# Gate units of block 2 as pairs of half-size products, with gates and results kept in DRAM

## The chip, the core and the metric

The kernel runs on one core of a Trainium2 chip. The metric is device time in microseconds, the median of several runs; lower is better.

## The reference, cut to what matters

Two blocks of two layers each run one after the other on 512 tokens of width 1024, in fp32. The change touches the second block. Its layer normalises the tokens and (in the first layer, for its output too) 256 context tokens, multiplies them with one wide matrix, runs three branches on parts of the product, and merges them:

```python
def merge_branches(ys, gm, w_br, w_out):
    y = jnp.stack(ys, axis=2)
    proj = jnp.einsum('btnw,nwd->btnd', y, w_br)
    g = jax.nn.sigmoid(gm.reshape(gm.shape[:2] + (N_BRANCH, -1)))
    return jnp.sum(g * proj, axis=2) @ w_out
```

Here `ys` are the results of branch a (differential attention, 4 heads), b (a bidirectional mLSTM, 4 heads) and c (neighbourhood attention, 4 pairs of heads), each 512 wide, and `gm` is a part of the wide product, 3 x 1024 columns: the gates.

## The kernel before, in words

Activations lie transposed: channels on the partitions, tokens on the free axis. A unit is 128 output channels, its weights one load of 512 KB. To keep fp32 accuracy, every operand is split in a high half of the type float32r and a low half (the rest); `mm3` (line 587) makes three matmuls per 128 channels of depth: high with high, high with low, low with high. So a unit over 1024 channels is 24 matmuls per block of up to 512 tokens. The normalised tokens are kept in `H` and `L` (high and low), 512 tokens and 256 of context. In layer 0 (`full`) a gate unit covers all 768, in layer 1 only the 512. `wload` (line 571) brings weights: a DMA on SyncE's queue into a buffer ws, a copy to the high half wh on ScalarE, a subtraction to the low half wl on VectorE; there are three buffers of each.

Block 2 (`run`, line 1817) goes through twelve heads in the order c, a, b. Each has a preparation and an attending (or scanning) generator. `weave` (line 492) runs the attending of one head beside the preparation of the next, in fixed proportions, and further generators beside them: `first` (the mLSTM's gates) and, by the table `MERGE` (line 1139), units of `merge` (line 1698). A unit of `merge` is a gate unit, its tanh on ScalarE and `branch_sum` (line 1721): 12 matmuls per block of tokens with the branch's weights (256 KB), multiplied with the gate and added to the sum `mg`. For branches c and a, 16 units stand beside heads 7 to 11; the 8 of branch b come after all heads. `out_proj` (line 1733) follows. Results of heads are split in high and low and stay in SBUF until their merge.

Working tiles come from the pool "s": 36 slots of 128 x 776 in block 2. PSUM tiles "P" are 8 banks.

What is written is not the order in which it is issued. `Order` (line 200) records every operation and in `flush` (line 371) orders them by a list schedule with modelled costs: each engine takes, of its first ready candidates in program order, the one that starts first, if its buffers are free; a tile may overtake others of its tag only by a set number (`AHEAD`, `WINDOW`). All instructions therefore carry line 486 (or 488, for runs that stay together) in the profile, and are told apart by their tiles: P is a PSUM tile, s a slot, wh and wl weights, H and L the split tokens.

Of the kernel before, what the change touches and what calls it, by code (L numbers as in the profile page):

```python
# [9 lines left out]
F32 = mybir.dt.float32  # L10
F32R = mybir.dt.float32r
I32 = mybir.dt.int32
AF = mybir.ActivationFunctionType
# [478 lines left out]
def weave(*gens):  # L492

    live = [[0.5 / n, 1.0 / n, g] for n, g in gens]
    while live:
        x = min(live, key=lambda x: x[0])
        x[0] += x[1]
        if next(x[2], live) is live:
            live.remove(x)


def chain(*gens):

    def run():
        for _, g in gens:
            yield from g
    return sum(n for n, _ in gens), run()


def some(g, n):  # L510

    for _ in range(n):
        next(g)
        yield

class Kern:
    WST = 3
# [30 lines left out]
    def part(self, o, n):  # L550
        return [self.H[:, k, o:o + n] for k in range(8)], [self.L[:, k, o:o + n] for k in range(8)]
# [19 lines left out]
    def wload(self, src, kt=8, m=128, parts=1):  # L571
        nc = self.nc
        self.n_ += 1
        w = kt * m
        st = nc.tile(self.wp, [128, 1088], F32, "wst", self.WST, f"ws{self.n_}")
        hi = nc.tile(self.wp, [128, 1088], F32R, "whi", 3, f"wh{self.n_}")
        lo = nc.tile(self.wp, [128, 1088], F32R, "wlo", 3, f"wl{self.n_}")
        src = src.rearrange("p k m -> p (k m)")
        for i in range(parts):
            r = slice(i * w // parts, (i + 1) * w // parts)  # L580
            nc.sync.dma_start(out=st[:, r], in_=src[:, r])
            nc.scalar.activation(hi[:, r], st[:, r], AF.Copy)
            nc.vector.tensor_tensor(lo[:, r], st[:, r], hi[:, r].bitcast(F32), op=ALU.subtract)
        return (hi[:, :w].rearrange("p (k m) -> p k m", k=kt),
                lo[:, :w].rearrange("p (k m) -> p k m", k=kt))

    def mm3(self, ps, w, xh, xl, order=None, start=True, stop=True):

# [547 lines left out]
VADD = (6, 7)  # L1136
FIRST = 7

MERGE = (0, 0, 0, 0, 0, 0, 0, 3, 3, 3, 4, 3)


class Block2:
# [83 lines left out]
    def source(self, name, j):  # L1226
# [4 lines left out]
            at += WN.get(u, 512) // 128  # L1231
        return self.A[f"w2in{self.l}"][at + j]

    def unit(self, name, j, lat, ctx):
        e = self.early.pop((self.l, name, j), None)
        if isinstance(e, list):
            return e
        return self.proj(self.source(name, j) if e is None else e, lat, ctx)
# [14 lines left out]
    def silu2(self, p):  # L1253

        nc = self.nc
        t = self.s(p[-1][1] + p[-1][2])
        for q, o, n in p:
            d = t[:, o:o + n]
            nc.scalar.activation(d, q, AF.Tanh, scale=0.5)
            nc.vector.scalar_tensor_tensor(d, d, 1.0, q, op0=ALU.add, op1=ALU.mult)  # L1260
        return t

    def ysplit(self, y, n):
        h, l = self.s(n, F32R), self.s(n, F32R)
# [15 lines left out]
    def head_out(self, o, ntile, g, gate):  # L1280

        K, nc = self.K, self.nc
        n = ntile * 128
        sq = self.s(n)
        b3 = lambda a: a.rearrange("p (a b) -> p a b", b=128)
        ss, v = K.tiny(ntile), K.tiny(ntile)
        nc.scalar.activation(sq, o, AF.Square)
        nc.vector.tensor_reduce(ss, b3(sq), axis=AX.X, op=ALU.add)
        nc.vector.tensor_scalar(v, ss, 1.0 / 128, EPS, op0=ALU.mult, op1=ALU.add)
        r = K.rsqrt(v, ntile)  # L1290
        nc.gpsimd.tensor_tensor(b3(o), b3(o), r.unsqueeze(2).to_broadcast([128, ntile, 128]), op=ALU.mult)
        for q, b, m in self.transposes(o, [i * 128 for i in range(ntile)]):
            d = gate[:, b:b + m]
            nc.vector.scalar_tensor_tensor(d, q, g, d, op0=ALU.mult, op1=ALU.mult)
        return self.ysplit(gate, n)


    def branch_a(self, lat, ctx, full, out):
# [50 lines left out]
        def attend(h):  # L1349
            st, vt = heads.pop(h)  # L1350
            nlam, gv = par
            o = self.s(ntile * 128)
            for t in range(ntile):
                isl = t < 4
                nk = 768 if isl else 256
                sm = K.tiny(4)
                mx = K.tiny(4)
                e = []
                for c in range(2):
                    S = K.pts(nk)  # L1360
                    for a, (q_, b, n) in enumerate(S):
                        k0 = b if isl else 512
                        K.mm_stack(q_, st[c], slice(t * 128, (t + 1) * 128), slice(k0, k0 + n))
                        nc.vector.tensor_reduce(mx[:, 2 * c + a:2 * c + a + 1], q_, axis=AX.X, op=ALU.max)
                    nm = K.tiny(1)
                    if isl:
                        nc.vector.tensor_scalar(nm, mx[:, 2 * c:2 * c + 1], mx[:, 2 * c + 1:2 * c + 2], -0.125,
                                                op0=ALU.max, op1=ALU.mult)
                    else:
                        nc.vector.tensor_scalar(nm, mx[:, 2 * c:2 * c + 1], -0.125, None, op0=ALU.mult)  # L1370
                    e.append(self.s(nk))
                    for a, (q_, b, n) in enumerate(S):
# [12 lines left out]
                O = K.pt(128)  # L1385
                for i in range(n):
                    nc.tensor.matmul(O, lhsT=pT[:, i * 128:(i + 1) * 128], rhs=vt[:, i if isl else 4 + i],
                                     start=(i == 0), stop=(i == n - 1))
                nc.scalar.activation(o[:, t * 128:(t + 1) * 128], O, AF.Copy)
                yield  # L1390
            z = self.silu2(self.unit("az", h, lat, cq))
            yield
            out.append(self.head_out(o, ntile, gv, z))

        return [((5 if h % 2 == 0 else 2, prep(h)), (ntile + 1, attend(h))) for h in range(4)]

# [80 lines left out]
    def branch_b(self, lat, ctx, full, out):  # L1477
# [33 lines left out]
        def scan(h):  # L1511
# [85 lines left out]
            out.append(self.head_out(o[0], ntile, gv, z))  # L1597

        return [((5 if h == 2 else 2, prep(h)), (6, scan(h))) for h in range(4)], (3, first())

# [1 line left out]
    def branch_c(self, lat, ctx, full, out):  # L1602
# [31 lines left out]
        def attend(j):  # L1634
# [58 lines left out]
            out.append(self.ysplit(y, nq))  # L1693

        return [((3, prep(j)), ((6 if full else 4) + 1, attend(j))) for j in range(4)]


    def merge(self, b, Y, mg, lat, ctx, full, last=False):


        K, nc, l = self.K, self.nc, self.l
        n = 768 if full else T
        cq = ctx if full else None
        late = []
        for m in range(8):
            t = self.s(n)
            for p, o, e in self.unit("gm", 8 * b + m, lat, cq):
                nc.scalar.activation(t[:, o:o + e], p, AF.Tanh, scale=0.5)
            late.append((mg, m, b, t, Y, n))
            if len(late) > (2 if last else 0):  # L1710
                self.branch_sum(*late.pop(0))
            yield
        for a in late:
            self.branch_sum(*a)
        if last:
            for m in range(8):
                h = K.H[:, m, :n]
                nc.scalar.activation(h, mg[m], AF.Copy, scale=0.5)
                nc.vector.scalar_tensor_tensor(K.L[:, m, :n], mg[m], 0.5, h.bitcast(F32), op0=ALU.mult, op1=ALU.subtract)
# [97 lines left out]
    def run(self, out, dbg, es):  # L1817
# [3 lines left out]
        for l in range(2):  # L1821
# [9 lines left out]
            early = chain((8, self.merge(2, yc, mg, lat, ctx, full)), (8, self.merge(0, ya, mg, lat, ctx, full)))[1]  # L1831
            weave(heads[0][0])
            for i in range(12):
                weave(heads[i][1], *([heads[i + 1][0]] if i < 11 else []), *([first] if i == FIRST else []),
                      *([(MERGE[i], some(early, MERGE[i]))] if MERGE[i] else []))
            weave((8, self.merge(1, yb, mg, lat, ctx, full, True)))
            X, S = self.out_proj(full, None if full or dbg == 6 else out)
            if dbg == 5 + l:
                for m in range(8):
# [43 lines left out]
```

## Time and profile before

| | us |
|---|---|
| median of 3 runs (lowest to highest) | 2919.61 (2916.12 to 2919.76) |
| the profiled execution | 2918.08 |
| its span, first to last instruction | 2916.3 |
| TensorE busy | 2868.6 |
| VectorE busy | 1876.1 |
| ScalarE busy | 1259.5 |
| GpSimd busy | 239.1 |

The first 1115 us or so are block 1; layer 0 of block 2 runs to about 2120 us, layer 1 to the end. The mean granted TensorE clock was 0.994 of full speed. A matmul's length in the profile is modelled and overlaps the next one's; the distance between starts is the rate. Idle time of an engine that is not the bottleneck costs nothing.

### The profile page before, as it was taken

How to read it: one execution, taken by the hardware profiler on the slowest of the kernel's cores; microseconds unless marked ns; L12 is line 12 of the kernel's file. 1: busy time of each engine (PE TensorE's matmuls, PEld its weight loads, DVE VectorE, ACT ScalarE, POOL GpSimd, SP SyncE). 2: the span in 40 equal slices, each digit the busy share in tenths (PEclk: the TensorE clock that was granted, in tenths of full speed). 3: DMA queues.
4: the chain of work that ended last, by engine and by line, in shares of the span. 5: the costliest groups of instructions: out<-in, count | busy, mean ns of one | idle time of the engine just before them, and what ended most of it. 6: DMA issues, size and time to landing. Idle time of an engine off the chain costs nothing.

```text
span 2916.3 us, 40946 instructions
## 1 busy us (share of the span) xinstructions
PE 2868.6 (98%) x15978; PEld 2432.4 (83%) x15978; DVE 1876.1 (64%) x3774; ACT 1259.5 (43%) x2405; POOL 239.1 (8%) x184
## 2 busy tenths in 40 slices
PE   8999999999999999999999999999999999999998
PEld 6788888887888888888888888888888888888887
DVE  7778678469786875656865554542466686565645
ACT  6344234455442443755554332322246555443324
POOL 1010000010100011000100101110100011011002
PEclk9999999999999999999999999999999999999999
DMA  4333433332334423111111212122222111132232
GB/s 148 119 120 129 136 133 118 104 102 81 129 110 140 141 94 123 66 64 44 37 34 41 87 56 66 60 89 71 91 95 82 45 58 42 66 95 79 87 105 87
DMA packets 94802, 260.58 MB, mean 89 GB/s; under 512 B 9608, under 2 KB 23304, under 8 KB 94608
## 3 DMA queue, kind: packets, MB, share of 16 engines
q1 hardware_dynamic: 94464, 257.96, 26.3%
q8 instruction: 125, 2.05, 0.3%
q14 instruction: 69, 0.57, 0.1%
q10 hardware_dynamic: 144, 0.00, 0.0%
HBM read 251.29 MB, written 6.64 MB: 88 GB/s over the span
## 4 chain that ended last, share of the span: by engine, by line
PE 92%; DVE 5%; DMA 1%; ACT 1%; issue 1%; POOL 0%; SPq 0%; DVEq 0%; ACTq 0%; POOLq 0%
PE P L486 91%; DVE s L486 2%; DVE t L486 1%; PE P L488 1%; DMA s<-cmd 1%; ACT s L486 1%; DVE tn L486 1%; DVE wl L486 1%; ACT wh L486 0%; DMA V<-in_vec 0%; DMA X<-in_x 0%; POOL t L486 0%; ACT t L486 0%; SPq L486 0%; DMA cmd<-s 0%
## 5 line engine op out<-in xcount | busy, mean ns | idle before, releaser
L486 PE MATMUL P<-H,wl 128*128 128x512 f32 (+1 forms) x2936 | 1079.6, 368 | 8.3 <-DVE wl L486 8.2
L486 PE MATMUL P<-H,wh 128*128 128x512 f32 (+1 forms) x2936 | 1081.2, 369 | 3.5 <-ACT s L486 1.9
L486 PE MATMUL P<-L,wh 128*128 128x512 f32 (+1 forms) x2936 | 1079.4, 368 | 1.5 <-DVE L L486 1.5
L486 ACT ACTIVATE wh<-ws 128x1024 fp32r<-128x1024 f32 (+4 forms) x426 | 412.1, 968 | 874.7 <-PE P L486 749.0
L486 DVE TENSOR_TENSOR wl<-ws,wh 128x1024 fp32r<-128x1024 f32 (+4 forms) x426 | 478.7, 1125 | 380.1 <-ACT wh L486 364.1
L486 PEld LDWEIGHTS P<-H,wl 128*128 128x128 f32 x2936 | 554.6, 189 | 104.7 <-DVE wl L486 10.3
L486 PEld LDWEIGHTS P<-H,wh 128*128 128x128 f32 x2936 | 554.5, 189 | 99.7 <-ACT s L486 3.0
L486 PEld LDWEIGHTS P<-L,wh 128*128 128x128 f32 x2936 | 554.2, 189 | 98.1 <-DVE L L486 3.2
L486 ACT ACTIVATE s<-P 128x512 f32<-128x512 f32 (+2 forms) x484 | 216.7, 479 | 330.6 <-PE P L486 307.3
L486 PE MATMUL P<-t,wh 128*128 128x512 f32 x960 | 301.3, 395 | 0.7 <-ACT t L486 0.7
L486 PE MATMUL P<-s,s 128*128 128x256 f32 (+4 forms) x1616 | 242.5, 290 | 6.0 <-DVE s L486 4.1
L486 PEld LDWEIGHTS P<-s,s 128*128 128x128 f32 (+1 forms) x1616 | 211.3, 188 | 31.2 <-ACT s L486 8.0
L486 PEld LDWEIGHTS P<-t,wh 128*128 128x128 f32 x960 | 180.6, 188 | 42.9 <-ACT t L486 0.9
L486 POOL TENSOR_TENSOR s<-s,s 128x512 f32<-128x512 f32 (+3 forms) x87 | 112.2, 1298 | 1155.2 <-DVE s L486 687.6
L486 PE MATMUL P<-t,wl 128*128 128x512 f32 x480 | 189.4, 395 | 0.0
L486 DVE TENSOR_REDUCE tn<-P 128x1 f32<-128x512 f32 (+1 forms) x224 | 105.9, 493 | 93.4 <-PE P L486 93.0
L486 DVE TENSOR_TENSOR s<-s,s 128x512 f32<-128x512 f32 (+6 forms) x173 | 148.4, 862 | 25.9 <-ACT s L486 12.3
L486 ACT ACTIVATE s<-s 64x768 fp32r<-64x768 f32 (+7 forms) x162 | 109.1, 680 | 119.0 <-DVE s L486 113.4
L486 PE MATMUL P<-s,wh 128*128 128x512 f32 (+1 forms) x576 | 155.6, 358 | 0.0
L486 DVE SCALAR_TENSOR_TENSOR t<-t,V,t 128x511 f32<-128x511 f32 (+1 forms) x196 | 148.3, 761 | 3.5 <-ACT t L486 1.6
L486 ACT ACTIVATE t<-t 128x512 f32<-128x512 f32 (+4 forms) x162 | 97.8, 611 | 112.1 <-DVE t L486 111.5
L486 PE MATMUL P<-wh,H 128*128 128x256 f32 (+2 forms) x512 | 145.9, 285 | 0.0
(142 smaller groups left out, 3114.8 us busy)
## 6 DMA issues: line engine op xcount, KB each, us to landing
ws<-in_w2in SPq DMA_DIRECT2D x136, 512.0 KB, 3.3
ws<-in_up SPq DMA_DIRECT2D x88, 512.0 KB, 3.2
wm<-in_w_mod SPq DMA_DIRECT2D x48, 512.0 KB, 4.2
ws<-in_down SPq DMA_DIRECT2D x32, 384.0 KB, 3.1
ws<-in_w2br SPq DMA_DIRECT2D x48, 256.0 KB, 2.6
ws<-in_down SPq DMA_DIRECT2D x32, 320.0 KB, 2.9
ws<-in_w0in SPq DMA_DIRECT2D x18, 512.0 KB, 3.4
ws<-in_w2out SPq DMA_DIRECT2D x16, 512.0 KB, 3.2
```

The source lines that it names most:

```text
L486: o["f"](*o["a"], **o["k"])
L488: f(*a, **k)
```

## The change

The 24 gate units of a layer are computed in pairs by a scheme with seven products in place of eight (Strassen's, in Winograd's form). The two units are the two halves of the output, the depth is cut in two halves of 512 channels and the tokens in two halves of n (384 in layer 0, 256 in layer 1). `halves`, once a layer, woven beside head 0, makes four combinations of token blocks (GpSimd restores fp32, VectorE subtracts, both split) and keeps them. `wpair` loads the pair's weights and makes four combinations of weight blocks on GpSimd. `pair` runs seven products of 12 matmuls of n columns, each added from PSUM on VectorE into the two outputs. `gm_pair` then takes the tanh and writes the gates to DRAM. The pairs stand beside heads 3 to 11 by the table `GM`. Results of branches c and a go to DRAM unsplit (`keep`). All three merges come after the heads: they load results and gates back and do the branch sums. There are four wh and wl buffers in place of three, and a smaller scratch for DMA descriptors of the GpSimd queue.

```diff
-        hi = nc.tile(self.wp, [128, 1088], F32R, "whi", 3, f"wh{self.n_}")
-        lo = nc.tile(self.wp, [128, 1088], F32R, "wlo", 3, f"wl{self.n_}")
+        hi = nc.tile(self.wp, [128, 1088], F32R, "whi", 4, f"wh{self.n_}")
+        lo = nc.tile(self.wp, [128, 1088], F32R, "wlo", 4, f"wl{self.n_}")
...
+    def wpair(self, srcs):
...
+        for i, src in enumerate(srcs):
+            st = nc.tile(self.wp, [128, 1088], F32, "wst", self.WST, f"ws{self.n_}_{i}")
+            nc.sync.dma_start(out=st[:, :1024], in_=src.rearrange("p k m -> p (k m)"))
+            raw.append(st)
...
+        sub = lambda o, x, y: nc.gpsimd.tensor_tensor(o, x, y, op=ALU.subtract)
+        put(raw[0], ("a11", "a12"))
+        sub(a11, a11, a21)
+        sub(s2, a22, a11)
+        put(s2, ("s2",), ("w2h", "w2l", 512, 1))
+        sub(a12, a12, s2)
+        put(raw[0], ("s3", "s4"))
+        nc.gpsimd.tensor_tensor(a21, a21, a22, op=ALU.add)
+        put(raw[1], ("s1", "a22"))
...
-MERGE = (0, 0, 0, 0, 0, 0, 0, 3, 3, 3, 4, 3)
+GM = (0, 0, 0, 1, 1, 1, 1, 2, 2, 2, 1, 1)
...
+    def halves(self, n):
...
+        for k in range(4):
+            x, y = self.s(2 * n), self.s(2 * n)
+            for a, r in ((x, k), (y, k + 4)):
+                nc.gpsimd.tensor_tensor(a, K.H[:, r, :2 * n].bitcast(F32), K.L[:, r, :2 * n].bitcast(F32), op=ALU.add)
...
+            nc.vector.tensor_tensor(b11, b12, b11, op=ALU.subtract)
+            nc.vector.tensor_tensor(b12, b22, b12, op=ALU.subtract)
+            nc.vector.tensor_tensor(b22, b22, b11, op=ALU.subtract)
+            nc.vector.tensor_tensor(b21, b21, b22, op=ALU.subtract)
+            for a, names in ((x, ("t1", "t3")), (y, ("t4", "t2"))):
+                h, l = self.ysplit(a, 2 * n)
...
+    def pair(self, srcs, o0, o1):
...
+        def part(a, b):
+            p = K.pt(n)
+            x = self.tk[b]
+            K.mm3(p, w[a], [q[0] for q in x], [q[1] for q in x])
+            return p
...
+        nc.scalar.activation(p1, part("a11", "b11"), AF.Copy)
+        yield
+        add(o0[:, n:], part("s2", "t2"), p1)
+        yield
+        add(o1[:, n:], part("s3", "t3"), o0[:, n:])
...
+    def gm_pair(self, b, m):
...
+        o = [self.s(2 * n) for _ in range(2)]
+        yield from self.pair([self.source("gm", 8 * b + m + i) for i in range(2)], *o)
+        for i in range(2):
+            nc.scalar.activation(o[i], o[i], AF.Tanh, scale=0.5)
+            nc.sync.dma_start(out=self.gd[b][:, m + i, :2 * n], in_=o[i])
+        yield
...
+    def keep(self, y, n, out, b):
+
+        if b == 1:
+            out.append(self.ysplit(y, n))
+        else:
+            self.nc.sync.dma_start(out=self.yd[b][:, len(out), :n], in_=y)
+            out.append(None)
...
         n = 768 if full else T
-        cq = ctx if full else None
-        late = []
+        for j in range(4):
+            if Y[j] is None:
+                y = self.s(n)
+                nc.sync.dma_start(out=y, in_=self.yd[b][:, j, :n])
+                Y[j] = self.ysplit(y, n)
         for m in range(8):
             t = self.s(n)
-            for p, o, e in self.unit("gm", 8 * b + m, lat, cq):
-                nc.scalar.activation(t[:, o:o + e], p, AF.Tanh, scale=0.5)
-            late.append((mg, m, b, t, Y, n))
-            if len(late) > (2 if last else 0):
-                self.branch_sum(*late.pop(0))
-            yield
-        for a in late:
-            self.branch_sum(*a)
+            nc.sync.dma_start(out=t, in_=self.gd[b][:, m, :n])
+            self.branch_sum(mg, m, b, t, Y, n)
...
+            gm = [self.gm_pair(b, m) for b in (2, 0, 1) for m in range(0, 8, 2)]
+            n = 384 if full else 256
             weave(heads[0][0])
             for i in range(12):
+                g = [gm.pop(0) for _ in range(GM[i])]
                 weave(heads[i][1], *([heads[i + 1][0]] if i < 11 else []), *([first] if i == FIRST else []),
-                      *([(MERGE[i], some(early, MERGE[i]))] if MERGE[i] else []))
-            weave((8, self.merge(1, yb, mg, lat, ctx, full, True)))
+                      *([(4, self.halves(n))] if i == 0 else []),
+                      *([chain(*((8, x) for x in g))] if g else []))
+            for b, y in ((2, yc), (0, ya), (1, yb)):
+                self.merge(b, y, mg, full, b == 1)
...
-    nc = bacc.Bacc("TRN2", target_bir_lowering=False, num_devices=1)
+    nc = bacc.Bacc("TRN2", target_bir_lowering=False, num_devices=1, dynamic_dma_scratch_size=1024)
```

## Rows read from the trace of the kernel before

**Rows 1.** The page's busy time: busy us, share of the span, instructions, by engine.

```profile
span 2916.3 us, 40946 instructions
PE 2868.6 (98%) x15978; PEld 2432.4 (83%) x15978; DVE 1876.1 (64%) x3774; ACT 1259.5 (43%) x2405; POOL 239.1 (8%) x184
```

**Rows 2.** The page's chain that ended last, by engine.

```profile
PE 92%; DVE 5%; DMA 1%; ACT 1%; issue 1%; POOL 0%; SPq 0%; DVEq 0%; ACTq 0%; POOLq 0%
```

**Rows 3.** Timeline of TensorE in layer 0: start us, modelled length us, instruction.

```profile
1899.92 0.40 PE L486 MATMUL P<-H,wh 128*128 128x512 f32 x1
...
1904.59 0.40 PE L486 MATMUL P<-H,wl 128*128 128x512 f32 x1
1904.82 0.28 PE L486 MATMUL P<-H,wh 128*128 128x256 f32 x1
...
1907.54 0.28 PE L486 MATMUL P<-H,wl 128*128 128x256 f32 x1
```

**Rows 4.** Stretches of heads: without merge work (first two), with it (last two).

```profile
core 0: us, PE busy (x) PEld busy (x) DVE busy (x) ACT busy (x) POOL busy (x), PEclk, DMA share, GB/s
1305.00:1505.00 200.00, 192.63 (x1325) 172.94 (x1325) 143.41 (x337) 107.80 (x273) 21.50 (x16) 0.99 0.12 41
2265.00:2440.00 175.00, 170.01 (x1145) 149.67 (x1143) 121.72 (x287) 94.41 (x234) 22.55 (x16) 1.00 0.15 52
1505.00:1950.00 445.00, 439.75 (x2759) 393.25 (x2758) 237.06 (x509) 151.99 (x328) 42.61 (x29) 1.00 0.19 63
2440.00:2755.00 315.00, 312.48 (x1741) 267.82 (x1742) 195.12 (x430) 132.12 (x278) 31.40 (x26) 1.00 0.23 75
```

**Rows 5.** Groups by form: a weight load.

```profile
L486 PEld LDWEIGHTS P<-H,wl 128*128 128x128 f32 x2936 | 554.6, 189 | 104.7 <-DVE wl L486 10.3 <-issue 1.2
```

**Rows 6.** Groups by form on VectorE, ScalarE, GpSimd: busy us, mean ns of one.

```profile
L486 DVE TENSOR_TENSOR wl<-ws,wh 128x1024 fp32r<-128x1024 f32 x304 | 374.5, 1232 | 236.9 <-ACT wh L486 225.1 <-PE P L486 9.0 <-ACT s L486 1.0
L486 DVE TENSOR_TENSOR wl<-ws,wh 128x512 fp32r<-128x512 f32 x52 | 38.1, 737 | 94.0 <-ACT wh L486 89.9 <-PE P L486 3.9
L486 DVE TENSOR_TENSOR s<-P,tn 128x384 f32<-128x384 f32 x16 | 8.2, 553 | 0.7 <-PE P L486 0.3 <-DVE tn L486 0.3
L486 DVE TENSOR_TENSOR s<-P,tn 128x256 f32<-128x256 f32 x16 | 6.1, 420 | 0.3
L486 DVE SCALAR_TENSOR_TENSOR s<-s,P 128x512 f32<-128x512 f32 x72 | 49.3, 685 | 68.0 <-PE P L486 48.0 <-ACT s L486 19.6
L486 ACT ACTIVATE wh<-ws 128x1024 fp32r<-128x1024 f32 x304 | 322.1, 1060 | 613.5 <-PE P L486 521.8 <-issue 88.1 <-ACT s L486 2.0
L486 ACT ACTIVATE wh<-ws 128x512 fp32r<-128x512 f32 x52 | 32.6, 630 | 111.9 <-PE P L486 95.0 <-issue 16.0 <-ACT s L486 0.9
L486 POOL TENSOR_TENSOR s<-s,s 128x512 f32<-128x512 f32 x53 | 73.7, 1394 | 940.3 <-DVE s L486 601.6 <-ACT s L486 163.3 <-DMA s<-xd 79.4
```

**Rows 7.** Timeline of GpSimd, then of VectorE, in layer 0.

```profile
1643.78 1.84 POOL L486 TENSOR_TENSOR s<-s,C 128x768 f32<-128x768 f32 x1 [1.03 <-DVE s L486]
1644.15 2.56 DVE L486 TENSOR_TENSOR wl<-ws,wh 128x1024 fp32r<-128x1024 f32 x1
```

**Rows 8.** DMA issues: KB each, median us to landing.

```profile
ws<-in_w2br SPq DMA_DIRECT2D x48, 256.0 KB, 2.6
s<-xd SPq DMA_DIRECT2D x16, 256.0 KB, 4.4
```

**Rows 9.** Groups by form on VectorE: making a head's stacked operands.

```profile
L486 DVE TENSOR_TENSOR s<-s,s 64x768 fp32r<-64x768 f32 x48 | 46.5, 969 | 3.1 <-ACT s L486 1.8
L486 DVE CAST s<-s 64x768 fp32r<-64x768 f32 x32 | 20.4, 665 | 0.7
```

**Rows 10.** Waits: who waited for whom, us in total, times, longest.

```profile
PE P L486 <- DVE wl L486: 8.2, 5, 3.4
SPq L486 <- DVE wl L486: 2039.8, 363, 28.2
```

More of the change, by code (lines that the diff above doesn't have):

```diff
@@ L507, in chain @@
     return sum(n for n, _ in gens), run()
-def some(g, n):
-    for _ in range(n):
-        next(g)
-        yield
 class Kern:
@@ L585, in wload, with put @@
                 lo[:, :w].rearrange("p (k m) -> p k m", k=kt))
+    def wpair(self, srcs):
+        nc = self.nc
+        self.n_ += 1
+        raw = []
+        for i, src in enumerate(srcs):
+            st = nc.tile(self.wp, [128, 1088], F32, "wst", self.WST, f"ws{self.n_}_{i}")
+            nc.sync.dma_start(out=st[:, :1024], in_=src.rearrange("p k m -> p (k m)"))
+            raw.append(st)
+        s2 = nc.tile(self.wp, [128, 512], F32, "w2", 1, f"w2{self.n_}")
+        a11, a12, a21, a22 = (raw[i][:, 512 * j:512 * j + 512] for i in range(2) for j in range(2))
+        out = {}
+        def put(x, names, tags=("whi", "wlo", 1088, 4)):
+            self.n_ += 1
+            n = 512 * len(names)
+            hi = nc.tile(self.wp, [128, tags[2]], F32R, tags[0], tags[3], f"wh{self.n_}")[:, :n]
+            lo = nc.tile(self.wp, [128, tags[2]], F32R, tags[1], tags[3], f"wl{self.n_}")[:, :n]
+            self.split(hi, lo, x[:, :n])
+            for i, a in enumerate(names):
+                out[a] = [y[:, 512 * i:512 * i + 512].rearrange("p (k m) -> p k m", k=4) for y in (hi, lo)]
+        sub = lambda o, x, y: nc.gpsimd.tensor_tensor(o, x, y, op=ALU.subtract)
[7 more added lines that the diff above has]
+        put(raw[1], ("s1", "a22"))
+        return out
     def mm3(self, ps, w, xh, xl, order=None, start=True, stop=True):
@@ L1232, in source @@
         return self.A[f"w2in{self.l}"][at + j]
+    def halves(self, n):
+        K, nc = self.K, self.nc
+        b = self.tk = {q: [] for q in ("b11", "b21", "b22", "t1", "t2", "t3", "t4")}
+        for k in range(4):
+            for nm, r, c in (("b11", k, 0), ("b21", k + 4, 0), ("b22", k + 4, n)):
+                b[nm].append((K.H[:, r, c:c + n], K.L[:, r, c:c + n]))
+        self.tn = n
+        for k in range(4):
+            x, y = self.s(2 * n), self.s(2 * n)
+            for a, r in ((x, k), (y, k + 4)):
+                nc.gpsimd.tensor_tensor(a, K.H[:, r, :2 * n].bitcast(F32), K.L[:, r, :2 * n].bitcast(F32), op=ALU.add)
+            b11, b12, b21, b22 = x[:, :n], x[:, n:], y[:, :n], y[:, n:]
+            nc.vector.tensor_tensor(b11, b12, b11, op=ALU.subtract)
[4 more added lines that the diff above has]
+                h, l = self.ysplit(a, 2 * n)
+                for i, nm in enumerate(names):
+                    b[nm].append((h[:, i * n:i * n + n], l[:, i * n:i * n + n]))
+            yield
@@ new lines, in pair @@
+    def pair(self, srcs, o0, o1):
+        K, nc, n = self.K, self.nc, self.tn
+        w = K.wpair(srcs)
+        def part(a, b):
[3 more added lines that the diff above has]
+            return p
+        add = lambda o, x, y: nc.vector.tensor_tensor(o, x, y, op=ALU.add)
+        p1 = self.s(n)
+        nc.scalar.activation(p1, part("a11", "b11"), AF.Copy)
[3 more added lines that the diff above has]
+        add(o1[:, n:], part("s3", "t3"), o0[:, n:])
+        yield
+        add(o1[:, :n], part("a22", "t4"), o1[:, n:])
+        yield
+        p = part("s1", "t1")
+        add(o0[:, n:], p, o0[:, n:])
+        add(o1[:, n:], p, o1[:, n:])
+        yield
+        add(o0[:, :n], part("a12", "b21"), p1)
+        yield
+        add(o0[:, n:], part("s4", "b22"), o0[:, n:])
@@ L1234, in unit @@
+    def gm_pair(self, b, m):
+        K, nc, n = self.K, self.nc, self.tn
+        o = [self.s(2 * n) for _ in range(2)]
[3 more added lines that the diff above has]
+            nc.sync.dma_start(out=self.gd[b][:, m + i, :2 * n], in_=o[i])
+        yield
     def unit(self, name, j, lat, ctx):
@@ L1294, in head_out @@
             nc.vector.scalar_tensor_tensor(d, q, g, d, op0=ALU.mult, op1=ALU.mult)
-        return self.ysplit(gate, n)
+        return gate
     def branch_a(self, lat, ctx, full, out):
@@ L1392, in attend @@
             yield
-            out.append(self.head_out(o, ntile, gv, z))
+            self.keep(self.head_out(o, ntile, gv, z), ntile * 128, out, 0)
         return [((5 if h % 2 == 0 else 2, prep(h)), (ntile + 1, attend(h))) for h in range(4)]
@@ L1596, in scan @@
             yield
-            out.append(self.head_out(o[0], ntile, gv, z))
+            self.keep(self.head_out(o[0], ntile, gv, z), ntile * 128, out, 1)
         return [((5 if h == 2 else 2, prep(h)), (6, scan(h))) for h in range(4)], (3, first())
@@ L1692, in attend, with merge @@
                 nc.vector.tensor_tensor(y[:, T:], o[:, T:], z[:, T:], op=ALU.mult)
-            out.append(self.ysplit(y, nq))
+            self.keep(y, nq, out, 2)
         return [((3, prep(j)), ((6 if full else 4) + 1, attend(j))) for j in range(4)]
-    def merge(self, b, Y, mg, lat, ctx, full, last=False):
-        K, nc, l = self.K, self.nc, self.l
+    def merge(self, b, Y, mg, full, last=False):
+        K, nc = self.K, self.nc
         n = 768 if full else T
-        cq = ctx if full else None
-        late = []
+        for j in range(4):
[3 more added lines that the diff above has]
+                Y[j] = self.ysplit(y, n)
         for m in range(8):
             t = self.s(n)
-            for p, o, e in self.unit("gm", 8 * b + m, lat, cq):
-                nc.scalar.activation(t[:, o:o + e], p, AF.Tanh, scale=0.5)
-            late.append((mg, m, b, t, Y, n))
-            if len(late) > (2 if last else 0):
-                self.branch_sum(*late.pop(0))
-            yield
-        for a in late:
-            self.branch_sum(*a)
+            nc.sync.dma_start(out=t, in_=self.gd[b][:, m, :n])
+            self.branch_sum(mg, m, b, t, Y, n)
         if last:
@@ L1830, in run @@
             mg = []
-            early = chain((8, self.merge(2, yc, mg, lat, ctx, full)), (8, self.merge(0, ya, mg, lat, ctx, full)))[1]
+            self.yd = {b: K.dr.tile([128, 4, 768], F32, name=f"yd{l}{b}") for b in (0, 2)}
+            self.gd = [K.dr.tile([128, 8, 768], F32, name=f"gd{l}{b}") for b in range(3)]
+            gm = [self.gm_pair(b, m) for b in (2, 0, 1) for m in range(0, 8, 2)]
+            n = 384 if full else 256
             weave(heads[0][0])
             for i in range(12):
+                g = [gm.pop(0) for _ in range(GM[i])]
                 weave(heads[i][1], *([heads[i + 1][0]] if i < 11 else []), *([first] if i == FIRST else []),
-                      *([(MERGE[i], some(early, MERGE[i]))] if MERGE[i] else []))
-            weave((8, self.merge(1, yb, mg, lat, ctx, full, True)))
+                      *([(4, self.halves(n))] if i == 0 else []),
+                      *([chain(*((8, x) for x in g))] if g else []))
+            for b, y in ((2, yc), (0, ya), (1, yb)):
+                self.merge(b, y, mg, full, b == 1)
             X, S = self.out_proj(full, None if full or dbg == 6 else out)
```

## The prediction

> **What bounds the kernel now.** I read the page's busy shares first, then the chain, then single matmuls, then the stretches of block 2. TensorE is busy for nearly the whole span, VectorE for under two thirds, GpSimd hardly [rows 1], and the chain that ended last runs through TensorE for 92% [rows 2]. "Busy" flatters it, since a matmul's modelled end overlaps the next one's start; what counts is the step from start to start. In a run of one unit, twenty steps of 512 columns go from 1899.92 to 1904.59 us, 233.5 ns each, and 23 steps of 256 columns from 1904.82 to 1907.54, 118.3 ns each [rows 3]. So a column costs 0.45 ns and the constant part is about 3 ns: time follows columns, and a change that streams fewer of them through TensorE saves time wherever TensorE stays fed. It is not quite fed in the attention heads: TensorE idles 7.4 of 200 us and 5.0 of 175 us in the stretches of heads without merge work, 5.3 of 445 us and 2.5 of 315 us in those with it [rows 4].
>
> **The products.** A pair of gate units was 48 matmuls of 512 columns, and in layer 0 another 48 of 256 for the context. Now it is seven products of 12 matmuls, 84, of 384 columns in layer 0 and 256 in layer 1. 384 columns lie midway between the measured steps: 175.9 ns. Layer 0: 48 x (233.5 + 118.3) = 16.89 us before, 84 x 175.9 = 14.78 after, 2.11 less; twelve pairs, 25.3 us. Layer 1: 48 x 233.5 = 11.21 before, 84 x 118.3 = 9.94 after; twelve pairs, 15.3 us. Together **40.6 us** off TensorE. The step of 118.3 ns is shorter than the 189 ns of one weight load [rows 5], and yet such a run has no gaps, so loads overlap and halving the columns is not punished. The Trainium skill (TensorE: Matmul & The Clock Gate, Back-to-back issue gap) gives sustained steps of about 81 ns at 128 columns and 131 ns at 512, set by both operations; a straight line between them would make small products poor and the net 6.5 us worse, an estimate from that page alone. The rows contradict it: 256 columns cost 0.51 of 512 here.
>
> **What is added beside it.** VectorE: a pair's splits are three of 1024 columns and one of 512, 3 x 1.232 + 0.737 = 4.43 us, plus seven adds from PSUM at 0.553 (384 columns) or 0.420 (256), so 8.3 or 7.4 us in place of 2 x 1.232; over 24 pairs that is 129 us. `halves` has 16 subtractions and eight 768- or 512-column splits per layer, by the same rows 16 and 13 us. Sum 158 us: from 64% to about 71% busy. ScalarE gets about 1.06 + 0.63 us of splits and one copy per pair, under 60 us in all, at 43% load. GpSimd gets 96 operations of 1.394 us and 16 wide ones, together about 162 us [rows 6]. None of this is on TensorE's path while products are queued for it, so I cost it at nothing by itself; if that cover is gone, it shows as below.
>
> GpSimd's work does reach VectorE. A split that takes 1.23 us took 2.56 us when it began behind a GpSimd operation of 1.84 us [rows 7]: it waited that one out. The Trainium skill (SBUF — State Buffer, Who interferes with whom) says that a VectorE instruction with two SBUF inputs and a GpSimd instruction that reads SBUF exclude each other for the whole instruction; the trace agrees. The adds read one operand from PSUM, where the mean for 512 columns is 0.685 us against 0.737 for a split of 512 [rows 6], so it is the splits and `halves` that are exposed.
>
> **Moved: the merges.** The 24 branch sums of a layer now stand behind all heads. Each is 12 matmuls per column block, 4.22 us in layer 0 and 2.80 in layer 1, unchanged in number. There VectorE has per unit a split, a gated product and an add: about 0.74 + 0.69 + 0.74 = 2.2 us in layer 1 and 3.0 in layer 0, and the H and L writes and split results of two branches once. In layer 1 that is some 63 us beside 67 us of TensorE: covered, barely. Loads are 256 KB of weights (2.6 us) and a gate tile (a like load, 4.4 us) [rows 8], three and many buffers deep. Bounds 0 to 10 us; I take 3, nearer the cover.
>
> **Moved: the fill.** Heads 7 to 11 had 16 merge units of 12.66 us (24 + 12 matmuls per block) in layer 0; now heads 3 to 6 get one pair each, 7 to 9 two, 10 and 11 one. Heads 3 to 6 lie in the stretches with 7.4 and 5.0 us idle; a pair there may fill 0 to 12 us of it, I take 5 back. Heads 10 and 11 lose fill: between nothing and the unfilled stretch's idle share, 3.7% of some 150 us per layer, 11 us in two layers; I take 4.
>
> **Slots.** The sums that `halves` makes are 16 of the 36 slots of the pool s, held from head 0 to the last pair. Finished results no longer stay (two slots per head), so from head 8 on the pool is no tighter than before, but in heads 0 to 2 it has up to 16 fewer and no pair to fill. A next head's operands (6 slots) may then come only as the current head's are freed. Their making is four subtractions of 0.969 us and four copies of 0.665 us on VectorE, 6.5 us [rows 9]. Six transitions, three per layer: between 0 (the unit of the head's own gate, 8.4 or 5.6 us of TensorE, stands just there) and 39 us. I take 6, near the cover. The pair also holds three of the four hi and lo weight buffers, so other units pass through one: 0 to 24 us at 1 us per pair; TensorE waits 8.2 us for the low halves in the whole trace now [rows 10], and a pair's own products can run meanwhile. I take 2.
>
> **DRAM trips.** Per layer SP issues 32 writes and 32 reads more. A write waits on its tanh with later weight loads queued behind it; but SP waits 2040 us in total for a weight buffer to come free [rows 10], so such a wait mostly replaces another. Cost taken 0, at most one landing (3 us) in a few places.
>
> **Sum.** The profiled execution took 2918.08 us (span 2916.3 and 1.8 around it), 1.5 under the median of the three runs. 2918.1 - 40.6 + 3 - 5 + 4 + 6 + 2 = 2887.5; against the median 2919.6 that is **2889 us**.
>
> **Rivals.**
> 1. *Slots bind.* In each of the six transitions without a pair, TensorE waits for the whole preparation: three evictions, the 6.5 us, a value transpose, about 10 us. 2918 - 40.6 + 60 + 1.5 = 2939, slower. It decides from (40.6 + 5.8) / 6 = 7.7 us per transition. For it: 16 slots of 36 are gone and VectorE is already 72% busy in the first unfilled stretch [rows 4]. Against it: before, the b heads ran with as many held (results and merge sums) and TensorE stayed 98.8% busy. 0.14.
> 2. *VectorE and GpSimd set the heads' pace.* 158 us more VectorE work and 162 us of GpSimd operations that can block it, 320 us over about 1700 us of block 2. If the idle of the head stretches (20 us in [rows 4]) more than doubles to give back 25 us beyond my 10: 2914, within the measurement's reach of no change. For it: [rows 7]. Against: TensorE's fill grows in the same heads. 0.14.
> 3. *Weight loads bind the half products*, 189 ns each: layer 0 saves 12 us, layer 1 loses 84 x 189 - 11,208 ns = 4.7 us twelve times, 56 us; 2964. The runs at 118.3 ns speak against it. 0.02. (The page named above makes small products dear as well, by a smaller sum.)
> 4. *Better:* the pairs fill all idle of their heads and nothing is given back: 2919.6 - 40.6 - 12 = 2867. 0.06.
>
> That the change does not do what it says has no room: all 24 units of each layer go through pairs.
>
> **Numbers.** Forecast 0.64 (2878 to 2902 by its own bounds). The range 2867 to 2920 takes in rivals 2 and 4, and leaves out 1 and 3. A measurement of this kernel tells about 0.2%, 5.8 us, from no change. Faster: the forecast, rival 4 and a part of rival 2 (0.04), 0.74; same: the rest of rival 2, 0.10; slower: rivals 1 and 3, 0.16.
>
> **What would show it.** The matmul groups of H with whole-gate weights lose 24 units per layer; groups of 128x384 and more of 128x256 appear, stepping 176 and 118 ns. TensorE's idle in heads 0 to 2 of each layer shows slots; the mean of two-input VectorE operations shows blocking; the last 100 and 67 us of each layer should be dense branch sums. I am wrong if half products step slower than 0.46 ns a column, or if head idle grows by over 30 us.

## The result, and the profile after

The changed kernel takes 2893.83 us, median of 4 runs (2892.04 to 2895.55), beside 2918.86 us for the kernel before on the same chip: a ratio of 0.9916 with a 95% interval of 0.9899 to 0.9933. It is faster by 25.0 us; 30.6 were forecast. The time lies inside the range, but two parts of the sum were wrong, and their errors cancel in part: the sums on GpSimd, put at nothing, cost time, and the new order, put at a small cost, cost none.

The page's busy time of the kernel after, as in [rows 1]:

```profile
span 2891.3 us, 42552 instructions
...
PE 2832.5 (98%) x16266; PEld 2444.7 (85%) x16266; DVE 2057.0 (71%) x4038; ACT 1308.7 (45%) x2469; POOL 402.3 (14%) x296
```

VectorE is at 71% and GpSimd has 163 us more, as forecast. The step of a half product is the one new number on TensorE; its timeline in layer 0 after (start us, modelled length us):

```profile
1324.36 0.34 PE L486 MATMUL P<-L,wh 128*128 128x384 f32 x1
...
1326.10 0.34 PE L486 MATMUL P<-H,wl 128*128 128x384 f32 x1
```

Ten steps from 1324.36 to 1326.10 are 174 ns each, against 175.9 read off between the two steps of [rows 3]. In layer 1 a product of 256 columns goes at the 118 ns of [rows 3] (twelve matmuls from 2338.44 us on, eleven steps in 1.29 us).

Where the time went is seen by layer: the stretch from the last matmul of block 1 to the last branch sum of layer 0, and from there to the last branch sum of layer 1. The stretches of before, then of after (columns as in [rows 4]):

```profile
1131.20:2074.50 943.30, 929.05 (x5997) 823.84 (x5996) 532.40 (x1203) 398.92 (x899) 74.87 (x52) 0.99 0.19 62
2074.50:2858.30 783.80, 775.97 (x4547) 665.34 (x4546) 478.66 (x1067) 353.52 (x750) 69.17 (x54) 1.00 0.23 78
```

```profile
1131.50:2050.10 918.60, 900.44 (x5853) 822.26 (x5852) 636.72 (x1333) 422.25 (x917) 160.56 (x108) 0.99 0.27 91
2050.10:2833.30 783.20, 767.37 (x4979) 680.27 (x4978) 561.57 (x1201) 379.02 (x795) 147.68 (x110) 1.00 0.30 100
```

Layer 0 is 24.7 us shorter: it kept nearly all of its 25.3. Layer 1 is 0.6 us shorter where 15.3 were due. TensorE's idle there went from 7.8 to 15.8 us; the rest hides under the modelled ends. An estimate from the starts in the two traces, with the median step of each matmul shape in the kernel before as the usual one: what layer 1's steps take beyond the usual grew by some 15 us. So the 15 us of the products were given back as lateness of TensorE's operands.

The two-input operations on VectorE tell where lateness comes from. Groups by form, after, as in [rows 6] (busy us, mean ns of one):

```profile
L486 DVE TENSOR_TENSOR wl<-ws,wh 128x1024 fp32r<-128x1024 f32 x328 | 417.1, 1273 | 153.5 <-ACT wh L486 149.2 <-PE P L488 2.8 <-issue 0.3
...
L486 DVE TENSOR_TENSOR s<-P,s 128x384 f32<-128x384 f32 x84 | 45.8, 553 | 19.1 <-PE P L486 18.5
...
L486 POOL TENSOR_TENSOR w<-ws,ws 128x512 f32<-128x512 f32 x24 | 34.3, 1429 | 0.0
...
L486 POOL TENSOR_TENSOR s<-H,L 128x768 f32<-128x768 f32 x8 | 18.1, 2295 | 34.1 <-DVE L L486 34.1
```

The split of 1024 columns has a mean of 1273 ns, 41 more than in [rows 6]; the add from PSUM is at its 553. A mean hides where the 41 lie. One place, layer 0 after, timeline of GpSimd and then of VectorE (start us, us, instruction, idle before it):

```profile
1289.00 1.41 POOL L486 TENSOR_TENSOR ws<-ws,ws 128x512 f32<-128x512 f32 x1 [116.04 <-DVE wl L486]
1290.48 1.34 POOL L486 TENSOR_TENSOR ws<-ws 128x512 f32<-128x512 f32 x1
1291.78 1.26 POOL L486 TENSOR_TENSOR w<-ws,ws 128x512 f32<-128x512 f32 x1
1293.12 1.33 POOL L486 TENSOR_TENSOR ws<-ws,w 128x512 f32<-128x512 f32 x1
```

```profile
1288.78 1.91 DVE L486 TENSOR_SCALAR s<-s,tn 128x512 f32<-128x512 f32 x2
1290.61 1.23 DVE L486 TENSOR_TENSOR tn<-tn 128x2 f32<-128x2 f32 x1
...
1292.07 2.65 DVE L486 TENSOR_SCALAR s<-s,tn 128x512 f32<-128x512 f32 x2
...
1298.25 0.16 DVE L486 TENSOR_TENSOR tn<-tn 128x2 f32<-128x2 f32 x1 [2.59 <-ACT s L486]
...
1298.65 0.88 DVE L486 TENSOR_SCALAR s<-s,tn 128x512 f32<-128x512 f32 x2
```

The four sums of a pair of weights run in one train on GpSimd. Beside it a sum of two columns on VectorE takes 1.23 us, and 0.16 a few microseconds later without it; a pair of scalings takes 1.91 and 2.65 us, and 0.88 alone. These belong to a head's normalisation, for which TensorE waits right there:

```profile
1293.47 0.63 PE L486 MATMUL P<-C,s 128*128 128x128 f32 x4 [1.77 <-DVE s L486]
```

At this place TensorE doesn't wait for the pair's weights; it waits for the attention's short steps, which the sums of the weights block. It isn't so everywhere: in block 2 the low half of a pair's own weights holds TensorE up three times, 4.1 us together, the longest in layer 0's mLSTM heads:

```profile
1708.02 0.44 PE L486 MATMUL P<-H,wl 128*128 128x384 f32 x1 [1.91 <-DVE wl L486]
```

The Trainium skill (SBUF — State Buffer, Who interferes with whom) has the rule: a VectorE instruction with two SBUF inputs, or one in a mode that takes both ports (scalings and copies can), and a GpSimd one that reads SBUF shut each other out for a whole instruction, while TensorE and ScalarE wait for nobody. The rows from 1288 us on agree in that VectorE's operations are held up beside GpSimd's. For ScalarE a run below bears on it.

### The profile page after: what moved, and what is told of

It is laid out like the page before. It is cut to its first block, busy times and chain, and to the rows that moved or that the text cites. A ratio compares the mean times of both kernels' runs of the same rounds, so it can differ in the third digit from the quotient of the medians.

```text
span 2891.3 us, 42552 instructions
## 1 busy us (share of the span) xinstructions
PE 2832.5 (98%) x16266; PEld 2444.7 (85%) x16266; DVE 2057.0 (71%) x4038; ACT 1308.7 (45%) x2469; POOL 402.3 (14%) x296
## 3 DMA queue, kind: packets, MB, share of 16 engines
q1 hardware_dynamic: 112896, 299.91, 30.6%
## 5 line engine op out<-in xcount | busy, mean ns | idle before, releaser
L486 PE MATMUL P<-H,wl 128*128 128x512 f32 (+2 forms) x2648 | 962.2, 364 | 8.2 <-DVE wl L486 8.2
L486 PE MATMUL P<-H,wh 128*128 128x512 f32 (+2 forms) x2648 | 963.9, 365 | 2.7 <-ACT H L486 2.6
L486 PE MATMUL P<-L,wh 128*128 128x512 f32 (+2 forms) x2648 | 962.4, 364 | 3.4 <-DVE L L486 3.4
L486 ACT ACTIVATE wh<-ws 128x1024 fp32r<-128x1024 f32 (+3 forms) x450 | 436.4, 972 | 765.0 <-PE P L486 660.3
L486 DVE TENSOR_TENSOR wl<-ws,wh 128x1024 fp32r<-128x1024 f32 (+3 forms) x450 | 522.1, 1162 | 208.2 <-ACT wh L486 203.1
L486 PE MATMUL P<-s,wh 128*128 128x256 f32 (+2 forms) x1344 | 329.7, 333 | 0.0
L486 ACT ACTIVATE s<-P 128x512 f32<-128x512 f32 (+3 forms) x436 | 189.9, 471 | 225.4 <-PE P L486 202.2
L486 PE MATMUL P<-s,s 128*128 128x128 f32 (+4 forms) x1616 | 246.6, 292 | 12.8 <-DVE s L486 12.7
L486 PEld LDWEIGHTS P<-s,wh 128*128 128x128 f32 x1344 | 228.9, 188 | 17.3
L486 PE MATMUL P<-s,wl 128*128 128x256 f32 (+2 forms) x672 | 222.3, 331 | 2.2 <-DVE wl L486 2.2
```

The lines of the kernel that those rows point to most:

```text
L486: o["f"](*o["a"], **o["k"])
```

## The experiments

The theory: the products' 40.6 us are real, and the sums given to GpSimd take a good part back by blocking VectorE (`pool`). The rivals: the sums of `halves` in head 0 do it (`slots`), or the new order with the merges at the end and the trips to DRAM does (`order`).

**One suspect at a time.** e1 to e4 stand against the same runs of before (median 2917.93); the changed kernel itself stood against runs with a median of 2918.86. Differences between runs of different sets carry up to 1.4 us from that.

e1: `halves` moves from head 0 to head 2, still ahead of the first pair.

```diff
-                      *([(4, self.halves(n))] if i == 0 else []),
+                      *([(4, self.halves(n))] if i == 2 else []),
```

> Theory (what is given back is lost in heads 0 and 1, where the combinations of token blocks take 16 slots and VectorE's and GpSimd's time with no pair beside them): made beside head 2 in place of head 0, TensorE's idle in the first two heads of either layer goes back to what it was before the change (in layer 1 under 1 us per 60 us, now 4.6), and the time falls by 6 to 12 us to about 2885. Rival 1 (the loss is in the thinner fill of the b heads and in the end of the layer): 2894, within 3. Rival 2 (the same work only disturbs another head): the idle of heads 0 and 1 goes, head 2's and 3's grows by as much, 2894 within 3.

Measured: 2886.43 us (2884.67 to 2888.35), ratio 0.9893 [0.9880, 0.9907], 7.4 us less than after. Layer 0 lost 0.4 us of it and layer 1 6.9. The place is layer 1's first head. TensorE and VectorE there, after:

```profile
2163.07 3.11 PE L486 MATMUL P<-s,s 128*128 128x256 f32 x15 [2.99 <-DVE s L486]
```

```profile
2142.88 3.23 DVE L486 TENSOR_TENSOR s<-s,s 128x256 f32<-128x256 f32 x2
...
2154.77 0.89 DVE L486 TENSOR_TENSOR s<-s,s 128x256 f32<-128x256 f32 x2
...
2157.04 0.68 DVE L486 TENSOR_TENSOR s<-s,s 128x512 fp32r<-128x512 f32 x1
2157.64 0.42 DVE L486 TENSOR_TENSOR s<-s 128x256 f32<-128x256 f32 x1
2158.16 1.36 DVE L486 TENSOR_TENSOR s<-s,s 128x256 f32<-128x256 f32 x3
...
2161.79 0.68 DVE L486 TENSOR_TENSOR s<-s,s 64x512 fp32r<-64x512 f32 x1
2162.50 0.76 DVE L486 CAST s<-s 64x512 fp32r<-64x512 f32 x2
```

VectorE is busy with the subtractions and splits of `halves` (128 partitions) and makes the stacked operands of the next head (64 partitions) only from 2161.79 on; TensorE waits 2.99 us for them. A part of VectorE's time there is again waiting for GpSimd, which makes the sums of high and low for the same `halves`:

```profile
2142.37 4.92 POOL L486 TENSOR_TENSOR s<-H,L 128x512 f32<-128x512 f32 x3 [1.02 <-DVE L L486]
```

Beside them two subtractions take 3.23 us, and 0.89 a little later. So the delay is VectorE's time, worked and waited; whether slots also ran short isn't told apart by this run. Layer 0, for which the same gain was expected, did not get it.

e2: layer 1 merges as before, with whole units beside the heads; only layer 0 has pairs.

```diff
+    def merge_old(self, b, Y, mg, lat, ctx, full, last=False):
...
-            for b, y in ((2, yc), (0, ya), (1, yb)):
+            for b, y in ((2, yc), (0, ya), (1, yb)) if full else ():
```

> Layer 1 is computed as in the kernel before, layer 0 as in the changed one. Theory (layer 0 kept its whole 25 us, layer 1 gave its 15.3 us back: between the ends of the two layers' branch sums lie 783.7 us before and 783.1 after): about 2894, within 3. Rival (layer 1 gains, and the mark between the layers misleads because work of layer 1 starts early): slower than the changed kernel by 8 to 15 us, 2902 to 2909.

Measured: 2894.85 us (2893.81 to 2898.77), 0.9925 [0.9913, 0.9938]. That is 1.0 us from the changed kernel: the whole change in layer 1 is worth about nothing, as the stretches said.

e3: order, DRAM trips and late merges stay, but `gm_pair` computes two whole units; no `halves`, no sums of weights.

```diff
-        yield from self.pair([self.source("gm", 8 * b + m + i) for i in range(2)], *o)
+        lat, ctx = K.part(0, T), K.part(T, TC)
+        for i in range(2):
+            for p, c, e in self.unit("gm", 8 * b + m + i, lat, ctx if self.l == 0 else None):
+                nc.scalar.activation(o[i][:, c:c + e], p, AF.Tanh, scale=0.5)
```

> Order, DRAM trips and late merges stay, but each pair is two whole units of 24 matmuls per block as before, and the combinations of token blocks are not made. Theory (the seven products are worth their 40.6 us, the combinations and the weights' preparation cost some 15 us of idle, moving and DRAM trips cost about nothing): 2918, within 5, as before. Rival 1 (the new order gains by itself, since heads 3 to 6 get fill): 2905 to 2912. Rival 2 (the new order and the DRAM trips cost the 15 us): 2928 to 2936.

Measured: 2913.97 us (2911.97 to 2916.73), 0.9987 [0.9978, 0.9996]: 4.0 us less than before. `order` falls as the loss: what is moved has, taken together, no cost that can be told. From here the products and what they bring along gave 20.1 of 40.6 us.

e4: the 96 sums of weights go to VectorE.

```diff
-        sub = lambda o, x, y: nc.gpsimd.tensor_tensor(o, x, y, op=ALU.subtract)
+        sub = lambda o, x, y: nc.vector.tensor_tensor(o, x, y, op=ALU.subtract)
...
-        nc.gpsimd.tensor_tensor(a21, a21, a22, op=ALU.add)
+        nc.vector.tensor_tensor(a21, a21, a22, op=ALU.add)
```

> The 96 subtractions and sums of weight blocks run on VectorE in place of GpSimd. Theory (GpSimd's blocking costs little on TensorE's path): 2894, within 3, with the mean of a two-input split of 1024 columns back near 1.23 us. Rival 1 (blocking is what is given back): faster by 5 to 10 us, 2884 to 2889. Rival 2 (VectorE is the bound in the heads, and 70 us more work on it shows): slower by over 5 us, 2899 or more.

Measured: 2876.92 us (2876.41 to 2877.99), 0.9862 [0.9847, 0.9877], 16.9 us less than after. The page and two groups by form of this kernel:

```profile
PE 2828.2 (98%) x16266; PEld 2443.5 (85%) x16266; DVE 2063.1 (72%) x4134; ACT 1310.6 (46%) x2469; POOL 268.7 (9%) x200
```

```profile
L486 DVE TENSOR_TENSOR wl<-ws,wh 128x1024 fp32r<-128x1024 f32 x328 | 406.2, 1240 | 160.1 <-ACT wh L486 156.9 <-PE P L486 1.4 <-issue 0.3
...
L486 DVE TENSOR_TENSOR ws<-ws,ws 128x512 f32<-128x512 f32 x24 | 16.5, 689 | 0.3
```

VectorE does 96 sums more, some 66 us at 0.689, yet its busy time rises by 6.1 us only: some 60 us of what counted as busy in the kernel after was VectorE waiting GpSimd out. (Summed over the kinds of instruction that both kernels issue in equal number, it is 51.) GpSimd also needs twice as long for the same sum, 1.33 to 1.43 us. Neither the theory (2894, within 3) nor rival 1 (5 to 10 us) had the size. The run takes two things away at once, the blocking and a slow chain that makes the weights; the next two runs part them.

**Is it the port or the amount?** e5, e6 and e7 share their runs of before (median 2917.50), e8, e9 and e10 theirs (2918.22). e5 takes e4 and adds 120 GpSimd sums of 384 columns that nobody waits for. e8 has the same 120 as copies on ScalarE.

```diff
+            j = nc.tile(self.wp, [128, 384], F32, "idle", 1, f"id{self.n_}")
+            for c in (0, n - 384) if "s3" in names else (0,):
+                nc.gpsimd.tensor_tensor(j, hi[:, c:c + 384].bitcast(F32), hi[:, n - 384:].bitcast(F32), op=ALU.add)
```

> As the run before with the weights' sums on VectorE, and beside them GpSimd does five sums of 384 columns per pair that read the finished high halves and that nobody waits for: some 5.3 us of GpSimd per pair, as much as in the changed kernel, but none of it in the chain that makes the weights. Theory 1 (GpSimd's work blocks VectorE's two-input operations, and that was the loss): back to 2888 to 2896. Theory 2 (the chain of four GpSimd operations in series, 5.6 us against 2.8 us on VectorE, holds weight buffers and comes late): stays at 2875 to 2880.

```diff
+                nc.scalar.activation(j, hi[:, c:c + 384].bitcast(F32), AF.Copy)
```

> As the run with idle sums on GpSimd beside the pairs, but the five operations of 384 columns per pair are copies on ScalarE: they read the same high halves and hold them as long, on an engine that has its own way into SBUF. Theory (VectorE was blocked by GpSimd's reading): 2876 to 2884, near the 2877 without any. Rival (what cost 23 us was that the weight buffers were held, or merely that the order shifted): 2890 to 2900.

Measured: e5 2900.46 us (2899.60 to 2903.19), 0.9940 [0.9927, 0.9952], 23.5 more than e4. e8 2878.78 us (2877.85 to 2880.22), 0.9866 [0.9852, 0.9881], 1.9 more. Page and groups of e5:

```profile
PE 2834.4 (98%) x16266; PEld 2446.1 (84%) x16266; DVE 2119.6 (73%) x4134; ACT 1310.4 (45%) x2469; POOL 447.4 (15%) x320
```

```profile
L486 DVE TENSOR_TENSOR wl<-ws,wh 128x1024 fp32r<-128x1024 f32 x328 | 427.7, 1306 | 142.1 <-ACT wh L486 139.3 <-PE P L486 1.2 <-issue 0.3
...
L486 POOL TENSOR_TENSOR id<-wh 128x384 f32<-128x384 f32 x120 | 177.3, 1478 | 682.9 <-ACT wh L486 677.1 <-DVE s L486 2.7
```

For comparison ScalarE's copy of 1024 columns in e5, 1060 ns as in [rows 6]:

```profile
L486 ACT ACTIVATE wh<-ws 128x1024 fp32r<-128x1024 f32 x328 | 346.5, 1060 | 530.9 <-PE P L486 440.3 <-issue 80.7 <-DVE ws L486 6.5
```

Then e8:

```profile
PE 2829.2 (98%) x16266; PEld 2446.2 (85%) x16266; DVE 2068.7 (72%) x4134; ACT 1361.3 (47%) x2589; POOL 266.3 (9%) x200
```

```profile
L486 ACT ACTIVATE id<-wh 128x384 f32<-128x384 f32 x120 | 62.6, 521 | 1.8
```

In e5 VectorE issues the same 4134 instructions as in e4 and is busy 56.5 us longer; nothing depends on the added sums but their own buffer. On ScalarE, copies at the same place leave VectorE's time and the kernel's nearly where they were. They hold the weight buffers for less time, though, 0.52 us each against 1.48, so e8 alone doesn't rule out held buffers; the trace of e5 does, for in it no engine's wait ends on an added sum. TensorE's longest waits, in e4 and then in e5 (us in total, times, longest):

```profile
PE P L486 <- DVE s L486: 16.1, 12, 3.9
PE P L486 <- DVE wl L486: 6.1, 4, 2.6
```

```profile
PE P L486 <- DVE s L486: 21.5, 22, 4.0
PE P L486 <- DVE wl L486: 13.4, 8, 3.4
PE P L486 <- POOL s L486: 6.3, 5, 1.8
```

The added waits end on VectorE's results, and five times on a sum of GpSimd's that a head needs. Before four of these five GpSimd had itself been idle for 1.9 to 4.7 us, waiting for VectorE, so it was not its own queue that was late. The one with the longest wait on TensorE's side:

```profile
2495.11 1.04 POOL L486 TENSOR_TENSOR s<-s,tn 128x512 f32<-128x512 f32 x1 [4.69 <-DVE tn L486]
```

```profile
2496.21 0.66 PE L486 MATMUL P<-C,s 128*128 128x128 f32 x4 [1.85 <-POOL s L486]
```

All this agrees with the rule of the Trainium skill above, for ScalarE by its unchanged 1060 ns; that TensorE itself isn't held up is not tested apart.

e5's 23.5 us are more than its theory allowed (2888 to 2896), and so is the work: 7.4 us of GpSimd per pair, not 5.3. Per microsecond of GpSimd's busy time it is 0.13 us of kernel in both directions: 16.9 us for 133.6 us taken away, 23.5 for 178.7 added. The two are not the same quantity, since the first is what is left after VectorE took over 66 us of sums.

**Together, and the noise of the order.** e6 is e4 with `halves` at head 2.

> Weights' sums on VectorE and the token combinations beside head 2. Theory (two losses at different places: the first heads of layer 1, and the pairs' weights in all later heads): both gains add, 2869, between 2866 and 2873. Rival (both remove the same idle): 2874 to 2878.

Measured: 2874.10 us (2872.48 to 2874.80), 0.9846 [0.9833, 0.9859]. With the weights' sums off GpSimd, moving `halves` is worth 2.8 us, not 7.4. That is 0.1 us inside the rival's bounds, and no more than order alone moves (below). By layers (table below) layer 1 still gains 5.2 us and layer 0 loses 3.1, so that the two gains are partly the same is not shown.

e7 is e6, and the 16 sums of high and low in `halves` go to VectorE too.

```diff
-                nc.gpsimd.tensor_tensor(a, K.H[:, r, :2 * n].bitcast(F32), K.L[:, r, :2 * n].bitcast(F32), op=ALU.add)
+                nc.vector.tensor_tensor(a, K.H[:, r, :2 * n].bitcast(F32), K.L[:, r, :2 * n].bitcast(F32), op=ALU.add)
```

> As the previous one, and the 16 sums of high and low token halves on VectorE too, so that the change adds nothing to GpSimd. If slow GpSimd operations in a chain are the loss wherever they stand: 2 to 5 us faster than the previous one. If VectorE's load in that head is what counts (11 us more on it per layer): 2 to 5 us slower.

Measured: **2867.89 us** (2866.72 to 2869.04), 0.9826 [0.9812, 0.9839], the best version: 26 us less than after, 50 less than before. It is 6.2 us faster than e6, the way of the first case and a little more than its 2 to 5; 5.6 of them lie in layer 0. Its page:

```profile
PE 2826.6 (99%) x16266; PEld 2441.3 (85%) x16266; DVE 2061.9 (72%) x4150; ACT 1311.3 (46%) x2469; POOL 235.9 (8%) x184
```

e9 is the kernel after with one modelled delay of the list schedule at 265 instead of 250. The work is the same, in another order.

```diff
-    LAG = {"pe": 190, "act": 230, "dve": 250, "pool": 250, "sp": 100}
+    LAG = {"pe": 190, "act": 230, "dve": 250, "pool": 265, "sp": 100}
```

> The changed kernel with one number of the list schedule's model altered (the lag after a GpSimd operation 265 ns in place of 250): the same work in a slightly other order. It measures how far the order alone moves the time. Theory (differences of over 5 us between the other runs mean something): 2894, within 4. Rival (the order alone moves it by as much as the edits did): over 5 us away from 2894.

Measured: 2889.82 us (2885.73 to 2891.91), 0.9903 [0.9886, 0.9919]: 4.0 us from nothing but order, with intervals that overlap. So differences of some 4 us between these kernels say nothing of a mechanism; and one such change is one sample, the reach of order may be larger. e4's 16.9 and e5's 23.5 are several times that; e1's 7.4 is under twice that, and stands on its row in layer 1 as much as on its time.

e10 is e7 with pairs from head 1 on and `halves` back at head 0.

```diff
-GM = (0, 0, 0, 1, 1, 1, 1, 2, 2, 2, 1, 1)
+GM = (0, 1, 1, 1, 1, 1, 1, 2, 2, 1, 1, 0)
```

> The kernel with nothing added to GpSimd, with the token combinations beside head 0 and pairs from head 1 on (0, 1, 1, 1, 1, 1, 1, 2, 2, 1, 1, 0). The idle that is left stands in heads 0 to 3 of either layer, about 25 and 20 us. Theory (those heads want fill): faster than 2868 by 4 to 10 us. Rival (the 16 slots, and three more for a pair, hold the heads' preparation up there, fill or not): 2868 to 2880.

Measured: 2870.88 us (2870.07 to 2871.82), 0.9839 [0.9824, 0.9854], beside 2918.22 for before. It is 3.0 us more than e7, within what order alone does: the 4 to 10 us expected did not come, and whether a better place for the pairs exists stays open. One place where e7 still idles is seen in the timeline of TensorE at the start of layer 1's mLSTM heads:

```profile
2555.84 0.49 PE L486 MATMUL P<-s,s 128*128 128x129 f32 x2 [0.98 <-DVE s L486]
...
2558.19 0.79 PE L486 MATMUL P<-s,s 128*128 128x129 f32 x4 [1.38 <-DVE s L486]
2560.08 1.20 PE L486 MATMUL P<-s,s 128*128 128x129 f32 x4 [1.11 <-DVE s L486]
```

The length of the two layers in each trace, between the marks named above:

| kernel | layer 0, us | layer 1, us |
|---|---|---|
| before | 943.0 | 783.7 |
| e3, no products | 944.0 | 778.2 |
| after | 918.3 | 783.1 |
| e1, halves late | 917.9 | 776.2 |
| e4, weights' sums on VectorE | 906.1 | 778.1 |
| e5, e4 and idle GpSimd sums | 918.3 | 790.7 |
| e6, e4 and e1 together | 909.2 | 772.9 |
| e7, all sums on VectorE | 903.6 | 772.3 |
| e8, e4 and ScalarE copies | 907.5 | 779.8 |
| e9, other order | 917.2 | 780.1 |

## Why the prediction was right, and where it was wrong

**The products: right in their steps.** 174 and 118 ns a step are what [rows 3] gave, and rival 3, loads of 189 ns as the bound, is out. From e3 to e7, with GpSimd's load as before, the products and what comes with them give 46.1 us, a little more than the 40.6. That likeness hides two misses: by layers it is 40.4 and 5.9 us, where 25.3 and 15.3 were due. So the sum alone proves nothing of the 40.6; the steps and the number of matmuls bear it.

**The step that failed** is "None of this is on TensorE's path while products are queued for it, so I cost it at nothing by itself". The sums on GpSimd cost 16.9 us for the weights (after to e4) and about 6 for `halves` (e6 to e7, near the reach of order). Rival 2 had the mechanism, with [rows 7] as its evidence, and set its price at 25 us; after is 25.9 above e7, in the three steps 6.2, 2.8 and 16.9. But it set the 25 on top of 10 for the order, slots and buffers, at 2914 us, 20 above what was measured, and it counted VectorE's added work too, which e7 has in full at the lowest time of all. The mistake was to ask only whether VectorE could carry its load, and to name as exposed only the splits and `halves`: at the place shown above it is the heads' own short operations that are blocked, and TensorE waits for them though pairs stand beside.

**Why it came out near all the same.** That is partly luck. Against the 40.6 us of the products 6 and 2 were set for slots and buffers and nothing for GpSimd, 8 in all; from e3 on, 20.5 us were given back, 12.5 more. The order, with merges and fill, was put at 3 - 5 + 4, in all 2 us of cost; e3 measured a gain of 4.0, 6 us better. The second error hides half of the first. A gain of 4.0 is not more than order's own noise, so merges, fill and DRAM trips have, together, no cost that can be told; their single sizes were not measured. At the layers' ends TensorE is dense; stretches of the kernel after (columns as in [rows 4]):

```profile
1980.00:2000.00 20.00, 20.00 (x117) 17.56 (x116) 10.75 (x18) 2.84 (x5) 0.00 (x0) 1.00 0.82 280
...
2800.00:2820.00 20.00, 20.00 (x88) 16.22 (x87) 14.37 (x23) 6.06 (x10) 0.00 (x0) 1.00 0.63 206
```

**Slots: the size about right, the reason not shown.** 6 us for slots and 2 for weight buffers were taken; moving `halves` gave 7.4 (2.8 with the weights' sums off GpSimd). The rows of e1 show VectorE late with the next head's operands because it works on `halves`; scarce slots show nowhere as a wait that could be told from it. Rival 1, 60 us of it, is out. TensorE's wait for low halves, 8.2 us in [rows 10], is 11.0 in the changed kernel and 6.1 in e4, in the waits of the kernel before (first line) and after (us in total, times, longest):

```profile
PE P L486 <- DVE s L486: 15.5, 12, 3.3
```

```profile
PE P L486 <- DVE s L486: 20.1, 20, 4.0
PE P L486 <- DVE wl L486: 11.0, 8, 2.6
```

**Rival 4** (2867) is not what the change does, but what e7 reaches: 2867.89.

**What stays open:** why the layers differ. Against e3 the changed kernel is 4.9 us longer in layer 1 and 25.7 shorter in layer 0; with all sums on VectorE (e7) it is 5.9 shorter in layer 1, 9 short of its due, and 40.4 in layer 0, 15 beyond. That layer 1 has shorter products to cover the same VectorE work is argued, not shown; no run changed it alone. Nor is it shown where layer 0's surplus comes from.

## What to carry to other kernels

Work put on GpSimd because it is idle is not free where VectorE feeds the bounding engine: here each microsecond of it went with 0.13 us of the kernel, and the same sums on the busier VectorE cost less, at half the duration. To price it, look for short operations on the path (a sum of two columns) and what they take beside a GpSimd instruction, rather than at shares of busy time; a busy time that falls short of the work added is waiting, counted as work. And before a difference is given a cause, change something that only reorders the work: here that alone moved 4 us.

## What the hardware showed that was not expected

- VectorE's busy time holds waiting: 96 sums more (66 us) raised it by 6.1 us once GpSimd's part was gone, and 177.3 us of GpSimd sums beside the same 4134 instructions raised it by 56.5 us.
- At the one place shown, the smallest operation suffers most in proportion: a sum of 128x2 took 1.23 us in place of 0.16. One-input scalings of 512 columns are held up too, a pair at 2.65 us in place of 0.88.
- 120 copies of ScalarE at the same place, 62.6 us, left VectorE's busy time within 5.6 us and the kernel within 1.9, and beside e5's GpSimd sums ScalarE's copy of 1024 columns stayed at 1060 ns.
